# A hybrid encoder layer on one core: later row stores, weight sums behind the block in front, and another price list for the lane planner

## The chip, the core and the metric

The kernel runs on one core of one Trainium2 chip. The engines are TensorE (PE, with its weight loads PEld), VectorE (DVE), ScalarE (ACT), GpSimd (POOL) and SyncE (SP), whose queue issues all the DMAs that are spoken of here. Each engine works off its own queue in the order in which the program wrote it. Times are device microseconds (us) of one execution; the metric is the median of several.

## The reference

One layer of a bidirectional encoder, all in fp32, on two groups of rows: 256 rows of a prompt and 1024 of a sample, together 1280 rows of 2048 features.

```python
def layer(x, mem, ...):
    hn = rms_norm(x, norm_g)
    proj = hn @ w_in                                  # 2048 -> 4896
    xbc, z_ssd, dt_raw, q, k, v, z_att, mq, z_mem = split_cols(proj, IN_SIZES)
    xbc = silu(centred_dwconv(xbc, conv_w, conv_b))
    ...                                               # two SSD scans, forward and backward
    o_ssd = rms_norm(y * silu(z_ssd))
    o_att = window_attention(q, k, v, sink) * silu(z_att)
    mk, mv = split_cols(rms_norm(mem, mem_norm_g) @ w_mem_kv, (512, 512))
    o_mem = (softmax over memory of mq, mk) @ mv * silu(z_mem)
    return x + concat([o_ssd, o_att, o_mem]) @ w_out  # 2048 -> 2048
```

Most of the arithmetic is in the three projections with w_in, w_mem_kv and w_out.

## The kernel before

**Split products.** PE's one-pass type is f32r. Each fp32 operand is split in two such parts: `wsplit` (line 337 of the kernel before) writes the high part `h` with a Copy on ACT and the rest `l` with a subtraction on DVE, and notes both instructions in `marks`. A product is then three matmuls, h·xH, h·xL and l·xH (or l and xL exchanged). In the trace the weights are `wraw` (as loaded), `wh` and `wl`; the rows of x are `ra` and `rb_` (as loaded), `xH` and `xL` (split).

**Stages.** The rows come in two groups of 640. The work goes through PE in this order, with the times of the trace:

1. Two blocks `mk` and `mv` from the memory rows (to about 75 us).
2. The block `q` of group 1 (to 153.5 us). A block takes 16 weight tiles of 128x512, five row tiles each. Beside it run the `p_step`s, which prepare the rows for the next stage: `p_load` (two loads of x), `p_fill` (norm on DVE, split to xH and xL, and two stores `rowH`, `rowL` of each of 16 row tiles to DRAM, from where a later stage reads them back), `p_sums` (four DVE subtractions), `p_split` (tH, tL of these sums).
3. `seven_stage(1)` (to about 423 us): ten units, each eight steps `k`, in which two blocks of weights and rows are multiplied with seven products in place of eight. This needs sums of weights: `weight_sums` loads a tile, makes four POOL operations (`ws`) and queues the result; `block_pair` splits tile and sums (`wh`, `wl` and `sh`, `sl`) and issues the matmuls. The five banks `acc` that the block in front has filled must be evicted (`qs`) before the third and later products can start.
4. Blocks `kv` and `q` of group 0 (to 495 us), then `seven_stage(0)` (to about 741 us).
5. The lanes (760 to about 1460 us): attention, SSD and memory work in small pieces, laid between the matmuls of six further blocks.
6. Blocks of w_out, and the seven-product stage of w_out from 1588 us to the end.

During the seven-product stages one `next(squares)` at four steps of a unit loads a piece of x to `sst` and squares it on ACT for the norm of group 0. Its tile and the first two weight tiles of a pair share a place in memory.

**What sets the order.** The instructions of an engine are put in order by a scheduler from priorities and simulated readiness; `tc.issue_after(ins)` makes what follows stand behind `ins`, but only on the engine of `ins`. So the `marks` bind ACT and DVE and not SP. The loads of the first two weight pairs are issued in `p_step` 23 and 25, ahead of the `issue_after` there. In the lane stage the order on PE is set by a planner, `Clocks`: `cost` gives each instruction a time, `ran` keeps a clock for each engine and the time at which each tile is full, and `ready` lets a lane go on when its inputs are due at most 300 ns (`AHEAD`) after PE's clock:

```python
at = [self.full.get(self.name(x), 0.0) - (0 if n else AHEAD) for x in tiles]
...
return max(at) <= self.now["PE"]
```

Every engine instruction of the kernel's own is recorded under one line of the recording helper, 128 (131 after the change), so groups are told apart by the names of their tiles.

Of the kernel before, what the change touches and what calls it, by code (L numbers as in the profile page):

```python
# [10 lines left out]
F32 = mybir.dt.float32  # L11
# [14 lines left out]
HP = (30, 100, 100)  # L26
# [5 lines left out]
RATES = {'kv': (4, 4), 'mq0': (8, 8), 'z0': (8, 8), 'z1': (8, 8), 'mq1': (8, 8), 'o': (8, 8)}  # L32
DEBT = 6.0
AHEAD, QUEUE = 300.0, 4000.0
NEG = -1e30

UNITS = (0, 4, 1, 5, 2, 6, 7, 3, 8, 9)
# [5 lines left out]
class Clocks:  # L43
# [17 lines left out]
    def cost(self, e, ins, ops, power):  # L61
        n = max([self.size(x) for x in ops] or [1])
        if e == "PE":
            m = self.size(ops[0])
            one_pass = ops[-1].dtype == F32R or ops[1].dtype == F32R
            return m / 2.4 + 14 if one_pass else max(m / 0.6, 213) + 6
        if e == "DVE":
            return 150 + 1.05 * n
        if e == "ACT":
            return (190 + 0.8 * n if n > 16 else 190) + (190 if len(ins.outs) > 1 else 0)  # L70
        if e == "POOL":
            return 60 + 4.2 * n if n > 16 else 250 + 180 * n if power else 300
        return 50

    def ran(self, e, ins, power=False):
        outs, srcs = [[x.bass_ap for x in xs if hasattr(x, "bass_ap")] for xs in (ins.outs, ins.ins)]
        cost = self.cost(e, ins, outs + srcs, power)
        if e != "SP":
            self.now[e] = max(self.now[e], self.now["PE"])
        if not self.lane:  # L80
            self.now[e] += cost
            return
        at = self.now[e] if e != "SP" else self.now["PE"]
        for x in srcs:
            at = max(at, self.full.get(self.name(x), 0.0))
        for x in outs:
            at = max(at, self.free.get(self.name(x), 0.0))
        if e == "SP":
            end = at + 2600 + self.size(outs[0]) * 1.5
        else:  # L90
            end = self.now[e] = at + cost + 20
        for x in srcs:
            k = self.name(x)
            self.free[k] = max(self.free.get(k, 0.0), end)
        for x in outs:
            k = self.name(x)
            if e != "SP":
                self.free[k] = max(self.free.get(k, 0.0), end)
            self.full[k] = end + 90
# [51 lines left out]
def hymba_encoder_kernel(  # L151
# [8 lines left out]
    V, A, G, T, S = [Timed(clk, n, e) for n, e in (("DVE", nc.vector), ("ACT", nc.scalar), ("POOL", nc.gpsimd),  # L160
                                                  ("PE", nc.tensor), ("SP", nc.sync))]
# [69 lines left out]
    row_d = [[dram([P, 640], f"row{n}{k}") for n in "HL"] for k in range(KT)]  # L231
# [28 lines left out]
            lanes[lane].append(((fn.__name__, t), fn(t)))  # L260

    marks = []

    def step(i):
        name, gen = lanes[i][0]
# [45 lines left out]
    cur = {}  # L311
# [31 lines left out]
    def w_laid(src, n):  # L343

        def load(k, raw):
            S.dma_start(raw, src[k])
        return load, n

    def laid_in(name):
# [861 lines left out]
    raw, sums, rows = {}, {}, {}  # L1211
# [46 lines left out]
    for k in range(8):  # L1258
        at = 2 * k - 5 if k < 4 else 4 * k - 13 if k < 7 else 13

        end = 16 if k == 7 else at
# [64 lines left out]
    def block_pair(src, u, rows_of, begin, lead=1):  # L1326

        ps = {p: (acc.tile([P, 512], F32, tag="acc", name="acc") if i < 5 else psum("accm"))[:, :320]
              for i, p in enumerate(seven)}
        parts = {}  # L1330
        for k in range(8):
            weight_sums(src, 8 * u + k + lead)
            with tc.high_priority(offset=HP[2]):
                raw, sums = ahead.pop(0)
                h = [wp.tile([P, 512], F32R, tag="wh", name="wh", bufs=WB),
                     fin.tile([P, 384], F32R, tag="sh", name="sh", bufs=3)]
                l = [wp.tile([P, 512], F32R, tag="wl", name="wl", bufs=WB),
                     fin.tile([P, 384], F32R, tag="sl", name="sl", bufs=3)]
                wsplit(raw, h[0], l[0])
                wsplit(sums, h[1], l[1])  # L1340
            parts[k] = h, l
            if k == 2:
                evac = begin(u)
            if k == 6:
                continue
            ks = (6, 7) if k == 7 else (k,)
            for p, (i, m, c) in seven.items():
                for k_ in ks:
                    h, l = [x[i][:, m * P:(m + 1) * P] for x in parts[k_]]
                    xh, xl = rows_of(k_, p, c)  # L1350
                    T.matmul(ps[p], h, xh, start=(k_ == 0), stop=False)
                    T.matmul(ps[p], h, xl, start=False, stop=False)
                    T.matmul(ps[p], l, xh, start=False, stop=(k_ == 7))
                if k == 7:
                    with tc.high_priority(offset=HP[2]):
                        evac(p, ps[p])
            yield k
# [20 lines left out]
    def p_fill(k, grp):  # L1378

        for i, x in enumerate(raw[k]):  # L1380
            g_ = R_G + k + 8 * i
            V.scalar_tensor_tensor(out=x, in0=x, scalar=vec[:, g_:g_ + 1], in1=rbc, op0=ALU.mult, op1=ALU.mult)
            h, l = new_place(k + 8 * i)
            A.activation(h, x, AF.Copy)
            V.tensor_sub(l, x, h.bitcast(F32))
            if grp == 1:
                for d, y in zip(row_d[k + 8 * i], (h, l)):
                    S.dma_start(d, y.bitcast(F32))

    def p_sums(k):  # L1390
        a, b = [hv(x, 2) for x in raw[k]]
# [19 lines left out]
    def p_step(j, grp):  # L1411
        if j == (3, 9)[grp]:
            need(x_rows, [1 - grp])
        if j in (23, 25):
            weight_sums(w_in_pairs, (j - 23) // 2)
        with ExitStack() as st:
            for ins in marks:
                st.enter_context(tc.issue_after(ins))
            for f, k, *args in sorted(p_plan[grp].get(j, ()),
                                      key=lambda x: ((p_split, p_sums, p_fill, p_load).index(x[0]), x[1])):  # L1420
                f(k, *args)
# [168 lines left out]
    def distances(_):  # L1590
# [7 lines left out]
        V.scalar_tensor_tensor(out=dist, in0=dist, scalar=-1.0, in1=dist, op0=ALU.mult, op1=ALU.min)  # L1598
        G.affine_select(out=dist, in_=dist, compare_op=ALU.is_ge, fill=NEG, base=0,
                        pattern=[[1, 384]], channel_multiplier=-1)  # L1600
# [50 lines left out]
    def one_left():  # L1651
        if left:
            some_left()
# [11 lines left out]
    def seven_stage(grp):  # L1665
        owe = 0.0
        for u, unit in enumerate(units):
            for k in block_pair(w_in_pairs, u, rows_in, ev_seven(*unit, grp), lead=2):
                if k in (0, 2, 4, 5):
                    next(squares, None)  # L1670
                owe = owe + 1.15 if left else 0.0
                while owe >= 1:
                    owe -= 1
                    one_left()
                if u == 0:
                    p_step(32 + k, grp)

    def both(k, j):
        one_left()
# [180 lines left out]
```

## Time and profile before

| what | value |
|---|---|
| median of 3 runs | 1793.35 us (1791.46 to 1794.4) |
| the profiled execution | 1788.47 us |
| its span (first to last instruction) | 1786.8 us |
| PE busy | 1762.2 us, 99% |
| DVE, ACT, POOL busy | 1302.3, 974.9, 668.4 us |
| DMA | 313.23 MB, mean 175 GB/s |

The profile lists an instruction as its start, its length, engine, line, operation, the tile written <- the tiles read, the shape and, in brackets, how long the engine stood idle before it and what ended that. "x2" stands for two of the same in a row. A time in brackets is idle time of that engine alone; for the kernel's time only PE's count directly, with 99% of the span. A stretch of the span is listed with its length, the busy time of the engines, the granted clock of PE (1.00 is full), the mean share of time in which the DMA engines were busy, and GB/s. Because matmuls are pipelined, a matmul's length there is longer than the distance from one to the next.

### The profile page before, as it was taken

The numbers are of one execution on the slowest core, as the hardware profiler recorded it, in microseconds if no ns is written. First come the engines' busy times: TensorE is split into PE (matmuls) and PEld (weight loads), VectorE is DVE, ScalarE is ACT, GpSimd is POOL, SyncE is SP. The second block draws the span as 40 slices with busy tenths as digits, with TensorE's granted clock in tenths as the row PEclk, the third lists the DMA queues.
The fourth block names the chain that finished last, engine by engine and source line by source line (L and its number), as shares of the span: only waits on it lengthen the run. The fifth ranks groups of instructions, "written<-read, shape, count | busy, mean of one in ns | idle before, by whom it ended". The sixth has DMA issues, their size and how long they took to land.

```text
span 1786.8 us, 30971 instructions
## 1 busy us (share of the span) xinstructions
PE 1762.2 (99%) x10306; PEld 1574.1 (88%) x10306; DVE 1302.3 (73%) x2417; ACT 974.9 (55%) x2181; POOL 668.4 (37%) x1092
## 2 busy tenths in 40 slices
PE   9999999999999999999999999999999999999999
PEld 7778999999799999988778877877788888889999
DVE  5585788888958888787788777768776533766665
ACT  6554545554454444346778766657886533433433
POOL 0105788970158889421111001121110100058775
PEclk9999999999999999999999999999999999999999
DMA  8795454455443333366557876666885635644442
GB/s 297 236 309 177 140 140 144 127 146 180 146 148 106 103 118 109 100 200 199 155 162 243 258 248 185 218 199 221 249 254 164 207 115 149 209 136 147 148 142 78
DMA packets 210993, 313.23 MB, mean 175 GB/s; under 512 B 21584, under 2 KB 84368, under 8 KB 210832
## 3 DMA queue, kind: packets, MB, share of 16 engines
q1 hardware_dynamic: 210688, 311.19, 56.1%
q8 instruction: 81, 1.33, 0.3%
q14 instruction: 80, 0.66, 0.1%
q10 hardware_dynamic: 144, 0.06, 0.0%
HBM read 242.42 MB, written 68.75 MB: 174 GB/s over the span
## 4 chain that ended last, share of the span: by engine, by line
PE 81%; issue 6%; DMA 5%; DVE 4%; ACT 2%; POOL 1%; SPq 0%; DVEq 0%; ACTq 0%; POOLq 0%
PE acc L128 58%; PE accm L128 11%; PE py L128 2%; PE psc L128 1%; PE po L128 1%; DVE wl L128 1%; PE pst L128 1%; PE ppt L128 1%; DMA rf<-ac 1%; PE pmo L128 1%; PE pms L128 1%; PE pyf L128 1%; PE pyb L128 1%; DMA wraw<-in_w_in_pairs_dram 1%; DMA rb<-ac 0%
## 5 line engine op out<-in xcount | busy, mean ns | idle before, releaser
L128 PE MATMUL acc<-wh,xH 128*128 128x512 f32 (+1 forms) x1248 | 490.7, 394 | 4.2 <-ACT wh L128 3.7
L128 DVE TENSOR_TENSOR wl<-wraw,wh 128x512 fp32r<-128x512 f32 (+1 forms) x480 | 353.1, 740 | 173.9 <-ACT wh L128 169.8
L128 PE MATMUL acc<-wl,xH 128*128 128x512 f32 (+1 forms) x1248 | 475.1, 381 | 2.8 <-DVE wl L128 2.6
L128 PE MATMUL acc<-wh,xL 128*128 128x512 f32 (+1 forms) x1248 | 472.6, 379 | 0.0
L128 ACT ACTIVATE wh<-wraw 128x512 fp32r<-128x512 f32 (+1 forms) x480 | 291.7, 614 | 200.4 <-PE acc L128 125.7
L128 POOL TENSOR_TENSOR ws<-wraw 128x128 f32<-128x128 f32 x224 | 144.7, 646 | 400.4 <-DMA wraw<-in_w_in_pairs_dram 202.9
L128 PEld LDWEIGHTS acc<-wh,xH 128*128 128x128 f32 x1248 | 234.9, 188 | 51.1 <-issue 7.0
L128 PEld LDWEIGHTS acc<-wl,xH 128*128 128x128 f32 x1248 | 235.2, 188 | 48.7 <-issue 6.5
L128 PEld LDWEIGHTS acc<-wh,xL 128*128 128x128 f32 x1248 | 234.6, 188 | 44.5 <-issue 1.0
L128 ACT ACTIVATE sh<-ws 128x384 fp32r<-128x384 f32 x224 | 116.3, 524 | 275.6 <-POOL ws L128 132.3
L128 DVE TENSOR_TENSOR sl<-ws,sh 128x384 fp32r<-128x384 f32 x224 | 157.1, 704 | 136.8 <-ACT sh L128 134.8
L128 POOL TENSOR_TENSOR ws<-wraw,ws 128x128 f32<-128x128 f32 x224 | 153.4, 685 | 17.3
L128 POOL TENSOR_TENSOR ws<-ws,wraw 128x128 f32<-128x128 f32 x224 | 152.8, 682 | 0.0
L128 POOL TENSOR_TENSOR wraw<-wraw 128x128 f32<-128x128 f32 x224 | 134.9, 602 | 17.3
L128 PE MATMUL acc<-xH,wl 128*128 128x320 f32 x320 | 100.1, 313 | 1.7 <-DVE wl L128 1.4
L128 PE MATMUL acc<-tH,sh 128*128 128x320 f32 x320 | 99.1, 310 | 1.9 <-ACT qs L128 1.9
L128 PE MATMUL acc<-tH,sl 128*128 128x320 f32 x320 | 99.2, 310 | 0.0
L128 PE MATMUL acc<-xL,wh 128*128 128x320 f32 x320 | 98.9, 309 | 0.0
L128 PE MATMUL accm<-tH,wl 128*128 128x320 f32 x320 | 98.8, 309 | 0.0
L128 PE MATMUL acc<-xH,wh 128*128 128x320 f32 x320 | 98.7, 309 | 0.0
L128 PE MATMUL accm<-tL,wh 128*128 128x320 f32 x320 | 98.7, 308 | 0.0
L128 PE MATMUL accm<-tH,wh 128*128 128x320 f32 x320 | 98.7, 308 | 0.0
(458 smaller groups left out, 3833.0 us busy)
## 6 DMA issues: line engine op xcount, KB each, us to landing
wraw<-in_w_in_pairs_dram SPq DMA_DIRECT2D x160, 256.0 KB, 2.7
wraw<-in_w_in_laid_dram SPq DMA_DIRECT2D x128, 256.0 KB, 3.6
wraw<-in_w_out_laid_dram SPq DMA_DIRECT2D x64, 256.0 KB, 3.0
wraw<-in_w_out_pairs_dram SPq DMA_DIRECT2D x64, 256.0 KB, 2.9
rf<-ac SPq DMA_DIRECT2D x40, 256.0 KB, 3.8
rb<-ac SPq DMA_DIRECT2D x40, 256.0 KB, 4.1
wraw<-in_w_mem_laid_dram SPq DMA_DIRECT2D x32, 256.0 KB, 4.4
ra<-in_x_turned_dram SPq DMA_DIRECT2D x16, 320.0 KB, 3.2
```

Source lines behind the costliest of these rows:

```text
L128: r = f(*a, **kw)
```

## The change

1. **Prices of the planner.** A vector operation of n columns costs 67 + 1.04 n ns in place of 150 + 1.05 n; a scalar one 50 (from PSUM) or 92 (from SBUF) + 0.835 n, in place of 190 + 0.8 n, and 92 for each further operand or accumulated output. The engine's clock goes on by that cost, and the result is there 90 (DVE) or 110 ns (ACT) later. Matmuls of more than one pass cost in proportion to their partitions.
2. **First weight sums.** `p_step` 23 and 25 issue the loads and sums of the first two weight pairs behind the `marks` and behind the last load of a laid weight block (`raws`, on SP).
3. **First splits of a seven-product stage.** In its unit 0, for k < 3, the splits are issued behind the marks of the block in front.
4. **Row stores.** `p_fill` issues none; `keep_rows` issues them one by one in units 2 to 9 of `seven_stage(1)`, behind `marks`.
5. **Squares.** At unit 0 and k = 0 and 2, no `next(squares)`.

```diff
+LATE = {"ACT": 110.0, "DVE": 90.0}
...
         if e == "PE":
...
-            return m / 2.4 + 14 if one_pass else max(m / 0.6, 213) + 6
+            return m / 2.4 + 14 if one_pass else max(m / 0.6, 213) * list(ops[0].ap)[0][1] / 128 + 6
         if e == "DVE":
-            return 150 + 1.05 * n
+            return 67 + 1.04 * n
         if e == "ACT":
-            return (190 + 0.8 * n if n > 16 else 190) + (190 if len(ins.outs) > 1 else 0)
+            aps = sum(hasattr(x, "bass_ap") for x in ins.ins)
+            return (50 if ops[-aps].space == "PSUM" else 92) + 0.835 * n + 92 * (aps - 1) + (92 if len(ins.outs) > 1 else 0)
...
-            end = self.now[e] = at + cost + 20
+            self.now[e] = at + cost
+            end = at + cost + LATE.get(e, 20)
...
     marks = []
+    raws = [None]
...
         def load(k, raw):
-            S.dma_start(raw, src[k])
+            raws[0] = S.dma_start(raw, src[k]).ins
...
+        front = tuple(marks) if u == 0 else ()
         for k in range(8):
             weight_sums(src, 8 * u + k + lead)
-            with tc.high_priority(offset=HP[2]):
+            with ExitStack() as st:
+                st.enter_context(tc.high_priority(offset=HP[2]))
+                for ins in front if k < 3 else ():
+                    st.enter_context(tc.issue_after(ins))
                 raw, sums = ahead.pop(0)
...
             V.tensor_sub(l, x, h.bitcast(F32))
-            if grp == 1:
-                for d, y in zip(row_d[k + 8 * i], (h, l)):
-                    S.dma_start(d, y.bitcast(F32))
...
-        if j in (23, 25):
-            weight_sums(w_in_pairs, (j - 23) // 2)
         with ExitStack() as st:
             for ins in marks:
                 st.enter_context(tc.issue_after(ins))
+            if j in (23, 25):
+                st.enter_context(tc.issue_after(raws[0]))
+                weight_sums(w_in_pairs, (j - 23) // 2)
...
-                if k in (0, 2, 4, 5):
+                if k in (0, 2, 4, 5) and (u or k > 2):
                     next(squares, None)
+                if grp == 1 and 2 <= u < 10 and k in (0, 2, 4, 7):
+                    keep_rows(4 * (u - 2) + (0, 2, 4, 7).index(k))
...
+    def keep_rows(i):
+
+        with ExitStack() as st:
+            for ins in marks:
+                st.enter_context(tc.issue_after(ins))
+            k, n = divmod(i, 2)
+            S.dma_start(row_d[k][n], cur["HL"[n], k].bitcast(F32))
```

What this does to the written order is seen at three places.

SP at the end of the q block of group 1, before and then after. `rowH_`, `rowL_` are the row stores, `wraw<-in_w_in_laid_dram` loads of the q block's weights, `wraw<-in_w_in_pairs_dram` loads for the seven-product stage, `sst` the first piece for the squares:

```order
L128 DMA rowH_224<-xH_1466 128x640
L128 DMA rowL_225<-xL_1467 128x640
L128 DMA rb__1473<-in_x_turned_dram 128x640
L128 DMA rowH_210<-xH_1519 128x640
L128 DMA rowL_211<-xL_1520 128x640
L128 DMA wraw<-in_w_in_laid_dram 128x512 x2
L128 DMA rowH_226<-xH_1526 128x640
L128 DMA rowL_227<-xL_1527 128x640
L128 DMA wraw<-in_w_in_pairs_dram 128x512 x4
L128 DMA sst<-in_x_sample_dram 128x512
L128 DMA q_143<-qs 128x512
```

The same place on SP after the change (the store `rowL_227`, a fourth pair load and `sst` follow):

```order
L131 DMA rowH_210<-xH_1491 128x640
L131 DMA rowL_211<-xL_1492 128x640
L131 DMA wraw<-in_w_in_pairs_dram 128x512
L131 DMA rowH_220<-xH_1268 128x640
L131 DMA rowL_221<-xL_1269 128x640
L131 DMA rowH_222<-xH_1335 128x640
L131 DMA wraw<-in_w_in_pairs_dram 128x512
L131 DMA rowL_223<-xL_1336 128x640
L131 DMA rowH_224<-xH_1440 128x640
L131 DMA wraw<-in_w_in_pairs_dram 128x512
L131 DMA rowL_225<-xL_1441 128x640
L131 DMA rowH_226<-xH_1496 128x640
```

All 32 row stores still stand ahead of the stage; the four pair loads, which stood behind them all, now stand among them.

ACT at the join between that q block and `seven_stage(1)`, before and then after. `wh` are weight splits, `sh` splits of weight sums, `qs` the evictions of the q block, `sst,xs` a Square:

```order
L128 ACTIVATE wh<-wraw 128x512
L128 ACTIVATE xH_1526<-rb__1473 128x640
L128 ACTIVATE wh<-wraw 128x512 x2
L128 ACTIVATE sh<-ws 128x384
L128 ACTIVATE tH<-ra 128x640
L128 ACTIVATE tH<-rb__1400 128x640
L128 ACTIVATE wh<-wraw_1388 128x512
L128 ACTIVATE qs<-acc 128x512 x2
L128 ACTIVATE sst,xs_1754<-sst 128x512
L128 ACTIVATE qs<-acc 128x512 x2
L128 ACTIVATE wh<-wraw_1451 128x512
L128 ACTIVATE wh<-wraw 128x512
```

The same join on ACT after the change:

```order
L131 ACTIVATE wh<-wraw 128x512 x4
L131 ACTIVATE sh<-ws 128x384 x3
L131 ACTIVATE wh<-wraw_1364 128x512
L131 ACTIVATE tH<-ra 128x640
L131 ACTIVATE qs<-acc 128x512
L131 ACTIVATE tH<-rb__1376 128x640
L131 ACTIVATE qs<-acc 128x512
L131 ACTIVATE sst,xs_1846<-sst 128x512
L131 ACTIVATE qs<-acc 128x512 x2
L131 ACTIVATE wh<-wraw_1427 128x512
L131 ACTIVATE wh<-wraw 128x512
L131 ACTIVATE qs<-acc 128x512
```

The splits `wh` of the q block now stand together ahead of all three `sh`; the Square stands between the second and the third eviction in both.

ACT at the join between the q block of group 0 and `seven_stage(0)`, with the same names, before and then after:

```order
L128 ACTIVATE wh<-wraw 128x512
L128 ACTIVATE sh<-ws 128x384
L128 ACTIVATE tH<-ra 128x640
L128 ACTIVATE xH_5816<-rb__5765 128x640
L128 ACTIVATE wh<-wraw 128x512
L128 ACTIVATE tH<-rb__5692 128x640
L128 ACTIVATE wh<-wraw 128x512
L128 ACTIVATE wh<-wraw_5674 128x512
L128 ACTIVATE qs<-acc 128x512 x2
L128 ACTIVATE sst,xs_4856<-sst 128x512
L128 ACTIVATE qs<-acc 128x512 x2
```

The second join on ACT after the change:

```order
L131 ACTIVATE wh<-wraw 128x512
L131 ACTIVATE xH_5811<-rb__5760 128x640
L131 ACTIVATE wh<-wraw 128x512 x2
L131 ACTIVATE sh<-ws 128x384 x3
L131 ACTIVATE wh<-wraw_5669 128x512
L131 ACTIVATE tH<-ra 128x640
L131 ACTIVATE qs<-acc 128x512
L131 ACTIVATE tH<-rb__5687 128x640
L131 ACTIVATE qs<-acc 128x512
L131 ACTIVATE sst,xs_6117<-sst 128x512
L131 ACTIVATE qs<-acc 128x512 x2
```

The two last `wh` of the q block, which stood behind `sh` and two `tH`, now stand ahead of them.

## The prediction

> **What bounds the kernel now.** I read the head of the page first, then the waits of PE, then the clock by stretch, and only then single instructions. TensorE (PE) is busy nearly all the time:
>
> ```profile
> span 1786.8 us, 30971 instructions
> PE 1762.2 (99%) x10306; PEld 1574.1 (88%) x10306; DVE 1302.3 (73%) x2417; ACT 974.9 (55%) x2181; POOL 668.4 (37%) x1092
> ```
>
> So there are 1786.8 − 1762.2 = 24.6 us of PE idle time, and no edit here removes a matmul. What can be won is a part of that idle time, and time that PE spends at a lower clock. The waits of PE over the whole span, largest first (total, times, longest), say where it idles, and the stretches below them (length, then busy time of PE, PEld, DVE, ACT, POOL, then granted clock, DMA share, GB/s) say where the clock fell:
>
> ```profile
> PE acc L128 <- DVE wl L128: 4.0, 6, 1.4
> PE acc L128 <- ACT wh L128: 3.7, 3, 1.6
> PE acc L128 <- ACT qs L128: 1.9, 1, 1.9
> PE ppt L128 <- DVE nm L128: 1.4, 1, 1.4
> ...
> 110.00:115.00 5.00, 3.53 (x16) 2.60 (x15) 2.61 (x4) 1.37 (x2) 0.00 (x0) 1.00 0.99 333
> 155.00:160.00 5.00, 3.47 (x12) 3.07 (x13) 1.30 (x2) 4.04 (x10) 0.02 (x1) 0.66 0.68 234
> 490.00:495.00 5.00, 4.30 (x11) 3.21 (x12) 1.91 (x3) 1.18 (x3) 3.55 (x7) 0.66 0.52 149
> 760.00:1590.00 830.00, 820.38 (x4385) 672.85 (x4384) 591.56 (x1290) 525.21 (x1344) 94.26 (x174) 1.00 0.64 199
> ```
>
> The reader is to see two things. The three largest waits are for the weight split (wh, wl) and for one eviction (qs). And in two stretches, which are the joins between a q block and the seven-product stage behind it, the clock is 0.66: (1 − 0.66) × 5 = 1.7 us is lost at each on top of the wait. The long lane stage idles 830 − 820.38 = 9.6 us, in a dozen small waits.
>
> [...]
>
> **Part A: the mk block (53 us).** PE waits twice there, because ACT stands at the sum split sh, which waits for POOL's weight sums of the first pair, and the block's own wh stands behind it:
>
> ```profile
> 52.00 0.53 ACT L128 ACTIVATE sh<-ws 128x384 fp32r<-128x384 f32 x1 [2.94 <-POOL ws L128]
> ...
> 53.09 0.50 PE L128 MATMUL acc<-wh,xH 128*128 128x512 f32 x1 [0.65 <-ACT wh L128]
> 54.28 0.50 PE L128 MATMUL acc<-wl,xH 128*128 128x512 f32 x1 [0.69 <-DVE wl L128]
> ```
>
> In the new order of ACT no sh stands in this block. The wh goes 2.94 us earlier at least in part; the gain is 0.65 + 0.69 = 1.34, with bounds 0 (another wait just behind) and 1.34. The two loads and eight POOL operations go to the q block instead. POOL has the room (gap of 73.66 us in the row under part C).
>
> **Part B: the q block (112 us).**
>
> ```profile
> 106.11 0.32 SPq L128 DMA_DIRECT2D rowL<-xL  x1
> 106.96 0.96 SPq L128 DMA_DIRECT2D wraw<-in_w_in_laid_dram  x1
> 111.71 0.63 ACT L128 ACTIVATE wh<-wraw 128x512 fp32r<-128x512 f32 x1 [3.19 <-DMA wraw<-in_w_in_laid_dram]
> 112.40 1.19 PE L128 MATMUL acc<-wh,xH 128*128 128x512 f32 x4 [1.47 <-ACT wh L128]
> ...
> rowL<-xL SPq DMA_DIRECT2D x16, 320.0 KB, 3.7
> ```
>
> The weight load is issued only after the row stores ahead of it on SP, which themselves wait for their splits, and it lands 4.75 us after issue, on a DMA that is 99% busy. In the new order this load stands ahead of those stores: −1.47. Against it: the 32 stores don't go to the seven-product stage. On SP they all still stand ahead of the first sst load and the q stores, and behind the last load of x there are now 14 of them where there were 4. Ten stores of 320 KB at 333 GB/s (row above) are 9.6 us of DMA time that comes later, in a stretch that has some 0.19 × 25 = 4.8 us free:
>
> ```profile
> 125.00:150.00 25.00, 25.00 (x112) 20.71 (x111) 17.79 (x31) 10.43 (x17) 4.07 (x8) 1.00 0.81 272
> ```
>
> The excess of about 5 us reaches the join unless the stores, which nobody waits for, give way to the loads. Bounds of B: −1.47 to +1.4 (a second wait like this one). I take −1.47, because most stores stand behind the loads that matter. The Squares that are dropped at the first unit go later into the seven-product stage, on an ACT that is busy 55% of the span (head of the page): 0, and without that cover 0.63 each (row at 155.15 below).
>
> **Part C: the first join (154 us).**
>
> ```profile
> 145.61 0.46 POOL L128 TENSOR_TENSOR ws<-wraw 128x128 f32<-128x128 f32 x1 [73.66 <-DMA wraw<-in_w_in_pairs_dram]
> 147.61 0.53 ACT L128 ACTIVATE sh<-ws 128x384 fp32r<-128x384 f32 x1 [3.41 <-POOL ws L128]
> 149.30 0.62 ACT L128 ACTIVATE wh<-wraw 128x512 fp32r<-128x512 f32 x1
> 155.15 0.63 ACT L128 ACTIVATE sst<-sst 128x512 f32<-128x512 f32 x1 [4.26 <-DMA sst<-in_x_sample_dram]
> 155.77 1.07 ACT L128 ACTIVATE qs<-acc 128x512 f32<-128x512 f32 x2
> 150.88 0.94 DVE L128 TENSOR_TENSOR wl<-wraw,wh 128x512 fp32r<-128x512 f32 x1
> 137.67 0.32 SPq L128 DMA_DIRECT2D rowL<-xL  x1
> 141.41 3.87 SPq L128 DMA_DIRECT2D wraw<-in_w_in_pairs_dram  x4
> 151.90 0.33 SPq L128 DMA_DIRECT2D sst<-in_x_sample_dram  x1
> 153.29 0.39 PE L128 MATMUL acc<-wh,xL 128*128 128x512 f32 x1
> 154.25 0.31 PE L128 MATMUL acc<-xH,wl 128*128 128x320 f32 x1
> 156.40 0.55 PE L128 MATMUL acc<-tH,sh 128*128 128x320 f32 x1 [1.85 <-ACT qs L128]
> ```
>
> Read backwards: PE waits for the third eviction (qs at 155.77); that stands behind a Square, which waits for its tile sst; the load of sst goes out at 151.90, when wl (150.88 + 0.94 = 151.82) has freed the buffer that both share; and wl waits for wh at 149.30, which stands behind sh and its POOL sums. The Square still stands between the second and third eviction afterwards. But the pair load that feeds the late sums is now issued among the stores instead of behind them all, so I put it at 138 instead of 141.41 (between the store at 137.67, behind which it now stands, and no change). Sums and sh come some 3.4 us earlier; wh is then held only by PE's release of a wh buffer (about 146.7: the 30 matmuls of the last two weights, 0.23 us apart by the rows at 487, before the block's end at 153.5), wl ends near 148.5, the load of sst goes out near 148.6 and, by the 3.25 us that it took (155.15 − 151.90), lands near 151.9. Square and the third eviction end near 153.1, ahead of PE's need at 154.4. Gain: 1.85 of idle time and 1.7 of clock, 3.55 in all. Bounds 0 and 3.55.
>
> **Part D: the second join (490 us).**
>
> ```profile
> 483.76 0.53 ACT L128 ACTIVATE sh<-ws 128x384 fp32r<-128x384 f32 x1 [3.28 <-POOL ws L128]
> 488.59 0.74 ACT L128 ACTIVATE tH<-rb__5692 128x640 fp32r<-128x640 f32 x1 [2.52 <-DVE rb__5692 L128]
> 489.23 1.14 ACT L128 ACTIVATE wh<-wraw 128x512 fp32r<-128x512 f32 x2
> 487.67 0.39 PE L128 MATMUL acc<-wl,xH 128*128 128x512 f32 x1
> 487.90 0.39 PE L128 MATMUL acc<-wh,xL 128*128 128x512 f32 x1
> 489.90 0.50 PE L128 MATMUL acc<-wh,xH 128*128 128x512 f32 x1 [1.62 <-ACT wh L128]
> 491.11 0.79 PE L128 MATMUL acc<-wl,xH 128*128 128x512 f32 x1 [0.70 <-DVE wl L128]
> ```
>
> The last weights of the q block (wh at 489.23) stand behind sh, two xH/tH splits and a wait for DVE. In the new ACT order the last two wh of the block stand ahead of the three sh and of the last two tH. That removes 1.62 + 0.70, and the clock's 1.7: 4.02. What is late next is sh and the tH splits, whose first reader on PE stands behind the 30 matmuls of the last two weights, 30 × 0.23 = 6.9 us; without that cover the 2.52 of the row at 488.59 would come back. Bounds 0 and 4.02. At the third join (the first w_out pair) the order of ACT does not change: 0.
>
> **Part E: the lanes.** The new estimate prices a 512-column vector operation at 67 + 1.04 × 512 = 599 ns of engine time and 689 until its result; the old one at 688 and 708. Rows of the lane stage (count, busy, mean ns):
>
> ```profile
> L128 DVE TENSOR_TENSOR state<-state,cd_all 128x512 f32<-128x512 f32 x24 | 16.4, 682 | 0.0
> L128 ACT ACTIVATE zs<-acc 128x512 f32<-128x512 f32 x20 | 11.8, 592 | 3.7 <-PE acc L128 3.7
> ```
>
> For an eviction of 512 columns it gives 50 + 427 + 110 = 587. So the new results' times fit the rows (682 and 592) within about 1%, and the lane matmuls move forward: 50 to 70 block matmuls by the order of PE, at 0.23 us each 11 to 16 us. Both queues have room (591.56 and 525.21 busy of 830). PE does the same matmuls and can only win or lose idle time: half of the 9.6 us gone is −5, doubled is about +9. I take 0, as an estimate that fits leaves the same margin of 300 ns that the planner had.
>
> **Sum.** 1.34 + 1.47 + 3.55 + 4.02 + 0 = 10.4. The profiled execution took 1788.47 (span 1786.8 and 1.67 around it), so 1778.1 for its like. The median of the runs, 1793.35, lies 4.9 above it: 1783.0.
>
> **The rivals.**
> - *The lanes wait more* (the other side). PE takes its matmuls in order, so each one placed before its input is ready stops all. For: the list of waits there consists of lane inputs (nm above, 1.4). Against: the fit of the prices. It decides when the lane idle time grows by over 10.4 + 3.6 = 14 us; at about 1 us each that is 14 new waits. It would give some 1797. Chance 0.08.
> - *The first join is not cured*: the Square stands where it stood and its load now follows a crowd of stores. For: the excess of 5 us; if sst lands 2 us later than I put it, the third eviction is late again. 1783 + 3.55 = 1786.5. Chance 0.17.
> - *The stores stay in the q block and crowd it*: part B gives nothing and one more wait of 1.4 comes: 1783 + 2.9 = 1785.9. For: the order of SP, and a DMA share of 0.99. Chance 0.13.
> - *The clock does not come back*: the half clock at the joins hangs on something else than these gaps (a gap of 1.47 at 112 us left it at 1.00): 1783 + 3.4 = 1786.4. Chance 0.03.
>
> [...]
> - *The lanes wait less*: 1778. Chance 0.1.
>
> **How the numbers follow.** The forecast has 0.49. Range: from 1776.5, a little under the lanes' gain, to 1790.5, where the second and third rivals come together with a loss of a few us in the lanes; only the first rival lies wholly outside. A difference of 0.2% (3.6 us) is what can be told: under 1789.8 is faster, above 1796.9 slower. All cases but the first rival end under 1789.8 taken alone (0.92); the spread of the median (1791.46 to 1794.4 now) and rivals that come together move 0.12 of it to no change, and the first rival gives 0.07 slower: 0.80, 0.13, 0.07.
>
> **What would show it.** A: no sh and no PE wait near 53 us. B: the wait at 112 us gone, and no other above 1 us up to 150. C: a clock of 1.00 around 155 us, with sst landed before 153. D: the same around 490. E: idle time of 7 to 12 us in the lane stage. The forecast is wrong if the clock is still 0.66 at a join, if the q block shows a new wait for a weight load, or if the lane idle time passes 15 us.

## The result, and the profile after

The change makes the kernel slower: 1801.06 us (1800.0 to 1804.0) against 1793.57 before, a ratio of 1.0047 with a 95% interval of 1.0034 to 1.0061. I had forecast 1783.0 and faster. The head of the page of the kernel after, and PE's longest waits over its span:

```profile
span 1801.4 us, 30978 instructions
PE 1766.0 (98%) x10306; PEld 1576.4 (88%) x10306; DVE 1311.5 (73%) x2417; ACT 972.1 (54%) x2181; POOL 683.7 (38%) x1092
```

```profile
PE pxs L131 <- DMA xc<-xbc_d: 4.7, 2, 3.7
PE po L131 <- ACT pT L131: 3.1, 2, 2.3
PE acc L131 <- ACT qs L131: 2.7, 3, 1.3
PE psc L131 <- ACT pT L131: 2.6, 2, 1.4
PE pacs L131 <- DVE dtw L131: 2.4, 1, 2.4
PE acc L131 <- DVE yt L131: 2.3, 2, 1.3
PE psc L131 <- DVE moT L131: 2.2, 1, 2.2
...
PE acc L131 <- ACT wh L131: 0.3, 1, 0.3
```

The weight splits, which led the list before (wl 4.0, wh 3.7), are gone from its head. The inputs of lane matmuls have taken their place. The two profiled executions side by side, each stage from its first block matmul on PE to that of the next stage (us):

| stage | before | after | difference |
|---|---|---|---|
| mk, mv and q blocks | 148.1 | 144.2 | −3.9 |
| first seven-product stage | 252.3 | 247.8 | −4.5 |
| kv and q blocks | 92.9 | 87.2 | −5.7 |
| second seven-product stage | 246.3 | 249.3 | +3.0 |
| lanes and w_out blocks | 838.9 | 865.0 | +26.0 |
| third seven-product stage | 198.8 | 198.6 | −0.2 |

Up to the start of the lanes the change wins 11.2 us (745.0 to 733.8); my sum said 10.4. This holds beyond the one profile: in the seventeen with edits 2 to 5 that are shown below the lanes begin between 732.8 and 736.9 us, in the two without them at 745.0 and 746.7. All of the gain, and more, is lost again in the lane stage. Stretches of the kernel after, with the columns of the prediction's fence:

```profile
49.00:54.00 5.00, 5.00 (x24) 4.14 (x23) 1.37 (x2) 1.48 (x3) 0.00 (x0) 1.00 0.80 247
112.00:117.00 5.00, 5.00 (x24) 4.14 (x23) 5.00 (x9) 3.50 (x6) 2.72 (x2) 1.00 0.96 316
152.00:157.00 5.00, 4.98 (x34) 4.98 (x35) 3.29 (x7) 2.91 (x7) 1.24 (x3) 1.00 0.53 194
485.00:490.00 5.00, 2.87 (x18) 2.30 (x17) 1.29 (x2) 3.74 (x8) 1.54 (x4) 1.00 0.55 210
733.80:1598.80 865.00, 839.49 (x4471) 688.82 (x4470) 595.44 (x1300) 526.42 (x1351) 95.03 (x170) 0.99 0.62 191
```

At 53 and 112 us PE is full, and at 152 us it is full again behind a last wait of 0.60; the clock is 1.00 in all three. At the second join (485 us) the clock is 1.00 as well, but PE is idle for 2.1 us of the five. In the lane stage PE is idle 865.0 − 839.49 = 25.5 us, where the same stage before had 838.9 − 830.5 = 8.4. The rest of the 26.0 is clock: in the lanes of this trace the clock is 0.50 from 807.14, 967.57 and 1203.09 us for 3.41 us each and from 1022.18 for 6.83, together 17.1 us at half clock, which cost 8.5 us, and in the kernel before it is 0.50 nowhere in this stage. The lane stage of the kernel before:

```profile
745.00:1583.90 838.90, 830.52 (x4470) 683.57 (x4469) 594.80 (x1299) 527.92 (x1351) 91.71 (x170) 1.00 0.64 197
```

Three of the 21 waits of this stage, followed back. First the matmul on PE, then the queue of the engine that it waits for:

```profile
967.31 1.75 PE L131 MATMUL po<-pT,v_all 128*64 128x256 f32 x6 [2.32 <-ACT pT L131]
...
964.05 1.28 ACT L131 ACTIVATE rf<-rf,wj_all 128x128 f32<-128x128 f32 x4 [1.85 <-DMA rf<-ac]
966.48 0.40 ACT L131 ACTIVATE rf<-rf,wj_all 128x128 f32<-128x128 f32 x1 [1.15 <-DMA rf<-ac]
966.79 0.85 ACT L131 ACTIVATE pT<-ppt 128x384 f32<-128x384 f32 x2
...
1202.85 0.51 PE L131 MATMUL psc<-kT,qT 128*128 128x384 f32 x1 [2.19 <-DVE moT L131]
...
1201.77 0.69 DVE L131 TENSOR_TENSOR q<-q,qr 128x512 f32<-128x512 f32 x1 [2.33 <-POOL qr L131]
1202.38 0.75 DVE L131 TENSOR_TENSOR moT<-pmo,zm 128x256 f32<-128x256 f32 x2
...
1016.10 0.58 SPq L131 DMA_DIRECT2D xc<-xbc_d  x1
1023.39 0.72 PE L131 MATMUL pxs<-identr,xc 128*128 128x128 f32 x4 [3.70 <-DMA xc<-xbc_d]
```

In the first, pT is ready to be evicted, but on ACT it stands behind an operation on `rf` whose load has not landed: the two loads of `rf` that ACT waits for took 4.0 and 4.6 us from issue to landing. In the second, moT stands on DVE behind an operation that waits for POOL. In the third, a load itself is late: issued at 1016.10, it landed 7.2 us later. None of them is a vector or scalar operation that took longer than its price. The three make 8.2 of the 25.5 us; the other waits were not followed back.

### The profile page after: what moved, and what is told of

Read it like the earlier page. It is cut to its first block, busy times and chain, and to the rows that moved or that the text cites. A ratio compares the mean times of both kernels' runs of the same rounds, so it can differ in the third digit from the quotient of the medians.

```text
span 1801.4 us, 30978 instructions
## 1 busy us (share of the span) xinstructions
PE 1766.0 (98%) x10306; PEld 1576.4 (88%) x10306; DVE 1311.5 (73%) x2417; ACT 972.1 (54%) x2181; POOL 683.7 (38%) x1092
## 4 chain that ended last, share of the span: by engine, by line
PE 82%; DVE 7%; DMA 6%; ACT 2%; issue 2%; POOL 1%; SPq 0%; DVEq 0%; ACTq 0%
PE acc L131 60%; PE accm L131 11%; PE py L131 2%; DVE wl L131 1%; DMA rf<-ac 1%; PE psc L131 1%; PE po L131 1%; PE pst L131 1%; PE pms L131 1%; PE pmo L131 1%; PE ppt L131 1%; DMA xc<-xbc_d 1%; PE pyb L131 1%; DMA rb<-ac 1%; DVE rb L131 1%
## 5 line engine op out<-in xcount | busy, mean ns | idle before, releaser
L131 POOL TENSOR_TENSOR ws<-wraw 128x128 f32<-128x128 f32 x224 | 152.6, 681 | 394.9 <-ACT rH L131 168.2
L131 POOL TENSOR_TENSOR es<-sinkb,nm 128x2 f32<-128x2 f32 x40 | 13.3, 333 | 226.5 <-DVE nm L131 197.1
```

The source lines that it names most:

```text
L131: r = f(*a, **kw)
```

## The experiments

All kernels compute the whole layer. The lane stage is given as length and PE's idle time in it, both from the profile; the position of the lane matmuls is their mean shift on PE against the kernel before, counted in block matmuls (minus is earlier), from the written order. A stage length is that of one profile, and half clock in it makes it longer (some 3.4 us in e8, none in e1, by mean clocks of 0.998 and 1.000 over the span). The kernel before, run beside each set, had medians of 1791.8 to 1793.7, so the ratio compares better than the time.

| kernel | shift | lane stage, idle (us) | time (us) | ratio, 95% interval |
|---|---|---|---|---|
| before | 0 | 838.9, 8.4 | 1793.4 | |
| after | −56 | 865.0, 25.5 | 1801.1 | 1.0034 to 1.0061 |
| e1 old prices | 0 | 840.3, 9.9 | 1779.4 | 0.9905 to 0.9943 |
| e2 prices only | −56 | 858.9, 23.2 | 1813.0 | 1.0092 to 1.0142 |
| e3 vector price old | +36 | 848.7, 16.1 | 1791.5 | 0.9976 to 1.0006 |
| e4 new, AHEAD −300 | −6 | 842.2, 11.5 | 1780.4 | 0.9913 to 0.9958 |
| e5 PE price new | +25 | 854.7, 18.0 | 1793.0 | 0.9989 to 1.0013 |
| e6 vector price new | −84 | 853.4, 16.7 | 1795.8 | 1.0001 to 1.0030 |
| e7 scalar price new | −2 | 853.3, 18.4 | 1791.2 | 0.9975 to 1.0003 |
| e8 old, no Square at joins | 0 | 842.0, 8.8 | 1777.1 | 0.9889 to 0.9942 |
| e9 old, AHEAD 350 | −4 | 845.7, 13.3 | 1784.0 | 0.9920 to 0.9950 |
| e10 old, AHEAD −300 | +58 | 848.1, 15.2 | 1787.8 | 0.9955 to 0.9990 |
| e11 new, AHEAD −400 | +28 | 860.4, 22.0 | 1798.7 | 1.0014 to 1.0050 |
| e12 scalar new, AHEAD −300 | +52 | 838.8, 7.6 | 1780.2 | 0.9901 to 0.9942 |
| e13 new, slow loads | +34 | 853.7, 17.6 | 1789.8 | 0.9974 to 1.0000 |
| e14 scalar new, slow loads | +72 | 843.4, 12.2 | 1781.3 | 0.9916 to 0.9953 |
| e15 PE new, slow loads | +89 | 841.4, 9.8 | 1781.1 | 0.9917 to 0.9953 |
| e16 vector new, slow loads | −30 | 851.3, 17.0 | 1789.1 | 0.9964 to 0.9993 |
| e17 e8, stores as before | 0 | 840.5, 10.2 | 1785.0 | 0.9950 to 0.9977 |
| e18 e8, stores truly later | 0 | 839.4, 9.2 | 1777.4 | 0.9897 to 0.9934 |

**Which half of the change costs: e1 and e2.** e1 is the change with the old prices:

```diff
-            return m / 2.4 + 14 if one_pass else max(m / 0.6, 213) * list(ops[0].ap)[0][1] / 128 + 6
+            return m / 2.4 + 14 if one_pass else max(m / 0.6, 213) + 6
-            return 67 + 1.04 * n
+            return 150 + 1.05 * n
... (the scalar price likewise)
-            self.now[e] = at + cost
-            end = at + cost + LATE.get(e, 20)
+            end = self.now[e] = at + cost + 20
```

> The change with the planner's old prices: edits 2 to 5 alone; the lane matmuls stand where they stood before. Theory (the lane loss comes from the prices alone, which put the lane matmuls on average 56 block matmuls earlier on PE): the joins and the q block keep the 11.2 us that the two profiles show up to the start of the lanes, the lane stage goes back from 865 to about 839 us, so some 11 us under the kernel before, about 1782. Rival (the lane stage pays for edits 2 to 5, because it starts earlier against its loads or with other row stores): the lane stage stays well above 845 us and the time at about 1800.

e2 makes the opposite edit: the same lines, the other way round, in the kernel before.

> The kernel before with the new prices alone. Theory: the lane stage loses all of its 26 us (17 of idle time and some 8.5 of half clock), nothing is won ahead of it: about 1793.5 + 26 = 1819. Rival: the prices alone cost under 8 us, about 1794 to 1801.

The lane stages of e1 and of e2:

```profile
734.60:1574.90 840.30, 830.45 (x4471) 684.09 (x4470) 595.50 (x1300) 526.39 (x1351) 91.81 (x170) 1.00 0.64 197
```

```profile
746.70:1605.60 858.90, 835.67 (x4470) 685.38 (x4469) 594.50 (x1300) 526.13 (x1350) 94.72 (x170) 1.00 0.62 193
```

With the old prices the stage is back at 840.3 us and the kernel at 1779.4, 14 us under the one before. The prices alone cost 20.0 us there and 19.6 in time (I expected 26). So the prices are the loss, and edits 2 to 5 the gain: 19.6 − 14.0 = 5.6 us, where the whole change costs 7.5.

**Which price: e3, e5, e6, e7.** Each has edits 2 to 5. e3 is the change with `return 150 + 1.05 * n` for DVE and its result 20 ns later, as before; the other three are e1 with one price of the change:

```diff
e5 -            return m / 2.4 + 14 if one_pass else max(m / 0.6, 213) + 6
e5 +            return m / 2.4 + 14 if one_pass else max(m / 0.6, 213) * list(ops[0].ap)[0][1] / 128 + 6
e6 -            return 150 + 1.05 * n
e6 +            return 67 + 1.04 * n      (result 90 later)
e7 -            return (190 + 0.8 * n if n > 16 else 190) + (190 if len(ins.outs) > 1 else 0)
e7 +            the change's scalar price  (result 110 later)
```

> The change with the old price and the old result time for vector operations alone (150 + 1.05 n, plus 20); the other new prices stay. On PE the lane matmuls then stand 36 block matmuls later than in the kernel before. Theory (the surplus in the old vector price was the margin of the lanes): lane idle time at or under that of before (8.4 us), no half clock, time 1778 to 1784. Rival (the loss hangs on the scalar price or on that of the matmuls of several passes): the lane stage stays above 855 us, the time near 1800.

> Edits 2 to 5 with the old prices, except that matmuls of several passes are priced by their partitions. Lane matmuls stand 25 block matmuls later on PE than before the change. Theory A (how far forward the lane matmuls stand decides): lane stage 836 to 841 us, time 1776 to 1780. Theory B (the old prices of PE and of the vector engine were both too high and stood against each other; any one of them put right alone makes the order worse, as the old vector price did in the kernel that kept the other new prices): lane stage 846 to 852 us, time 1786 to 1791.

> Edits 2 to 5 with the old prices, except that vector operations have the new price and result time. Lane matmuls stand 84 block matmuls earlier than before the change, farther than with all the new prices (56). Theory A: the lanes lose more than the 26 us of the full change: lane stage 870 to 885 us, time 1810 to 1825. Theory B: also worse than the old prices, by some 26 to 40 us. Against both: a lane stage of 840 to 850 us would say that the vector price is not what costs.

> Edits 2 to 5 with the old prices, except that scalar operations have the new price and result time. Lane matmuls stand where they stood (1.5 block matmuls earlier on average). Theory A: no loss, lane stage 838 to 843 us, time 1778 to 1782. Theory B (a margin in the scalar price guarded the matmuls that wait for the scalar engine, such as psc and po behind pT): lane stage 845 to 852 us, time 1785 to 1791.

Each single price makes the lane stage 13 to 14 us longer than the old prices do, whether the lane matmuls stand 25 later, 84 earlier or, with the scalar price, where they were on average. e3, with the old vector price and matmuls 36 later, still waits 16.1 us. My theory, that the loss grows with how much earlier the matmuls stand, falls. The lane stage of e6, the farthest move:

```profile
735.10:1588.50 853.40, 836.67 (x4470) 685.95 (x4469) 592.48 (x1300) 527.20 (x1350) 99.43 (x170) 0.99 0.63 194
```

**More margin: e4, e9 to e12.** The edit in each is one number:

```diff
-AHEAD, QUEUE = 300.0, 4000.0
+AHEAD, QUEUE = -300.0, 4000.0   (e4 in the change, e10 in e1, e12 in e7; e9: 350 in e1; e11: -400 in the change)
```

> The change with all its prices, but a lane goes on only when its inputs were due 300 ns ago, in place of up to 300 ns ahead (AHEAD -300 for 300). On PE the lane matmuls stand 6 block matmuls earlier than before the change on average, in place of 56. Theory (placement decides, by whatever means): most of the lane loss goes, lane idle time 8 to 14 us, time 1782 to 1790. Rival (an order of work made by the new prices that is bad in itself, or loads that come late, not the distance from an input to its matmul): still above 1796.

> Edits 2 to 5 with the old prices and a margin that is a little smaller: inputs may be due 350 ns ahead instead of 300. Lane matmuls stand 4 block matmuls earlier on PE on average, so every distance is nearly as it was, but the order is another one. Theory C (the order under the old prices was the one of many that happens to wait little, and any other costs some 13 us, as the three single prices did: 853 to 855 us of lane stage): 848 to 858 us, time 1788 to 1795. Theory D (the distance from an input to its matmul decides, and the single prices took some of it for their own engine's inputs): 839 to 845 us, time 1778 to 1784.

> Edits 2 to 5 with the old prices and 600 ns more margin: a lane goes on only when its inputs were due 300 ns ago. Lane matmuls stand 58 block matmuls later on average. Theory C: another order, so 848 to 858 us of lane stage, time 1788 to 1795. Theory D: more margin everywhere, 835 to 842 us, time 1774 to 1781.

> The whole change with its new prices and AHEAD at -400, 100 ns more margin than the kernel with -300 that came to a lane stage of 842 us. Theory C (842 was a chance find): 850 to 865 us, time 1788 to 1803. Theory D (with the true prices it is the margin that counts): 836 to 843 us, time 1775 to 1782.

> Edits 2 to 5, old prices except the new one for scalar operations, and AHEAD at -300. With 300 this kernel had a lane stage of 853 us, idle 18.4 us. Theory C: no different, 848 to 858 us, time 1786 to 1793. Theory D: the 600 ns take away most of the extra waits, 838 to 845 us, time 1777 to 1784.

e4 seemed to settle it: 600 ns more margin gave 842.2 us. But 100 ns more than that (e11) gave 860.4, and the same 600 ns under the old prices made the stage 7.8 us longer (e10 against e1), under the new scalar price 14.5 us shorter (e12 against e7). Neither margin nor position predicts the sign. A small change of margin (e9) costs 5.4 us, between what theories C and D said, and no more than two profiles of one order can differ (6.1, next). The same order repeats better than orders agree: before, e1, e8, e17 and e18 share one and lie at 838.9 to 842.0 us, the change and e2 share another at 865.0 and 858.9, and the thirteen further orders lie at 838.8 to 860.4.

**The price of loads: e13 to e16.** The loads that lanes wait for, in the kernel after between 760 and 1400 us (count, KB, median us from issue to landing):

```profile
rf<-ac SPq DMA_DIRECT2D x40, 256.0 KB, 4.1
rb<-ac SPq DMA_DIRECT2D x40, 256.0 KB, 4.3
...
xc<-xbc_d SPq DMA_DIRECT2D x18, 256.0 KB, 5.0
```

The planner gives each of them 2600 + 1.5 × 512 = 3368 ns, before and after the change. The edit, in the change (e13), e7 (e14), e5 (e15) and e6 (e16):

```diff
-            end = at + 2600 + self.size(outs[0]) * 1.5
+            end = at + 4600 + self.size(outs[0]) * 1.5
```

> The whole change with its new prices, and the planner's price of a DMA raised by 2.0 us (4600 + 1.5 n ns in place of 2600 + 1.5 n; for 512 columns 5.4 us in place of 3.4, where the loads xc, rb and rf took 5.0, 4.3 and 4.1 in the median). Theory E (the lanes wait because loads land later than the planner allows, and engines that stand in order behind such a load hold up others): lane stage 838 to 847 us in place of 865, time 1776 to 1786. Theory C (any new order gives a draw from the same 839 to 865 us, mean 851): around 851 us, time around 1790, and the four kernels of this set together as wide apart as the ten before.

> Edits 2 to 5, old prices except the new one for scalar operations, and DMAs priced 2.0 us higher. Without the latter the lane stage was 853 us. Theory E: 836 to 845 us, time 1775 to 1784. Theory C: a draw around 851 us, time around 1790.

> Edits 2 to 5, old prices except the new one for matmuls of several passes, and DMAs priced 2.0 us higher. Without the latter the lane stage was 855 us. Theory E: 836 to 845 us, time 1775 to 1784. Theory C: a draw around 851 us, time around 1790.

> Edits 2 to 5, old prices except the new one for vector operations, and DMAs priced 2.0 us higher. Without the latter the lane stage was 853 us. Theory E: 838 to 847 us, time 1776 to 1786. Theory C: a draw around 851 us, time around 1790.

All four stages got shorter: by 11.3, 9.9, 13.3 and 2.1 us, and in the ratios all four kernels are faster than without the edit, with intervals that don't touch. Two fall into theory E's range (843.4, 841.4), and these are the two with the old vector price. The two with the new one stay at 853.7 and 851.3. But the four don't decide between E and C. They began from orders that were worse than most, so that a mere new draw would help too: the eleven orders with the old price of loads have a mean of 850 us, these four one of 847, and by an estimate from those eleven, draws among the other ten would all four come out shorter about one time in three. That loads land later than they are priced is seen directly in two of the waits above (4.0, 4.6 and 7.2 us, against 3.4); that a right price makes a good order is not shown, nor that the vector price's surplus covers something else, which two kernels against two suggest. Against a simple sum stands that the old prices, with the low price of loads, wait as little as the best of these.

**The row stores and the Square: e8, e17, e18.** e8 is e1 without Squares in the first unit; e17 is e8 with the stores issued in `p_fill` again, as before the change; e18 is e8 with the stores bound on SP behind the latest pair load, so that they really go out in units 2 to 9:

```diff
e8  -                if k in (0, 2, 4, 5) and (u or k > 2):
e8  +                if u and k in (0, 2, 4, 5):
e17 +            if grp == 1:
e17 +                for d, y in zip(row_d[k + 8 * i], (h, l)):
e17 +                    S.dma_start(d, y.bitcast(F32))
e17 -                    keep_rows(4 * (u - 2) + (0, 2, 4, 7).index(k))
e18 +        pairs[0] = S.dma_start(raw, src[i // 8, i % 8]).ins
e18 +            st.enter_context(tc.issue_after(pairs[0]))
```

> Edits 2 to 5 with the old prices, and no Square is issued in the whole first unit of a seven-product stage, so none stands between the second and the third eviction at a join. What this tells: whether the two new waits for the evictions at the second join (1.31 and 0.82 us, a loss of 2.4 us) and the one of 0.60 at the first come from the Square, whose piece lands late. If so, both joins run through: 3.0 us less than the same kernel with the Square there (1779.4), about 1776.5. Rival (the evictions are late because the splits tH wait for the sums on DVE): the same waits stay, about 1779.

> The kernel without Squares at the joins and with the old prices (e8, 1777.1 us), with edit 4 undone: p_fill issues the row stores again. The lane matmuls stand where they stand there. If the gain of 1.47 us at 112 us comes from edit 4: that wait comes back, and the q block is 1.5 us longer, about 1778.6. If it comes from the edits 2 and 3 alone: 1777 and no wait above 1 us in the q block. My prediction's part B says the first.

> The same kernel (e8) with the row stores bound behind the pair loads on SP, so that they really go out in units 2 to 9 of the first seven-product stage, where the change in words wants them. If stores among the loads cost something in the q block or at the join: up to 1 us less than e8 ahead of that stage. If they are hidden anyway: the same, 1776 to 1778. Rival on the other side: in the seven-product stage they hold up pair loads and its length grows beyond 249.5 us.

In e8 the waits for evictions at the joins fall to one of 0.3 us in all, from 0.60 at the first and 1.31 + 0.82 at the second in the kernel after (2.8 in all in e1). So the Square made them. The time is 2.3 us under e1 where I said 3.0, but the intervals overlap, and in the two profiles the lanes begin only 1.0 us earlier: what this is worth is not shown. The two long waits of PE ahead of the lanes in e17:

```profile
111.41 1.21 PE L129 MATMUL acc<-wh,xH 128*128 128x512 f32 x4 [2.02 <-ACT wh L129]
146.54 1.63 PE L129 MATMUL acc<-wh,xH 128*128 128x512 f32 x4 [2.56 <-ACT wh L129]
```

```profile
111.00:116.00 5.00, 4.59 (x14) 3.67 (x15) 4.60 (x6) 2.76 (x5) 1.00 (x2) 0.70 0.86 298
146.00:151.00 5.00, 4.46 (x13) 3.51 (x14) 3.71 (x5) 3.01 (x6) 3.05 (x5) 0.66 0.50 154
```

Without edit 4 the kernel is 7.9 us slower than e8 (1785.0 to 1777.1): the wait at 111 us is there again, a second one of 2.56 comes at the end of the block, and each costs a stretch at half clock. I had said 1.5 us. So the edit carries more than half of what e8 gains over the kernel before (0.0049 of 0.0085 in the ratios). How far back the stores then go counts for nothing more. The stretch from 125 to 150 us in e8, and then in e18:

```profile
125.00:150.00 25.00, 25.00 (x114) 20.84 (x113) 16.66 (x24) 12.39 (x22) 10.33 (x16) 1.00 0.85 311
```

```profile
125.00:150.00 25.00, 25.00 (x112) 20.70 (x111) 17.62 (x25) 11.59 (x20) 8.96 (x14) 1.00 0.39 119
```

With the true move the DMA share there is 0.39 instead of 0.85 in e8, and the times are the same (1777.4 and 1777.1): the stores that stayed were hidden.

## Why the prediction was wrong

**Part A, right.** No sh and no wait stand at 53 us. A and B together were to bring 2.8 us up to the first join; they brought 3.9. Most of the further 1.1 lies in how a wait is listed: a matmul of 512 columns is listed 0.39 us long, but its neighbours start 0.23 apart, so PE loses more than the listed idle time. Counted from start to start, the three waits of the kernel before cost 3.6 us instead of 2.8. The last 0.3 is not traced.

**Part B, right in its sign and its edit, too small in what the edit is worth.** The wait at 112 us is gone, on a DMA that is still 96% busy. e17 shows that without edit 4 the other edits would not have kept that gain and would have met a second wait, which I had not priced. Its rival, stores that crowd the block, did not come.

**Part C, right in its sequence, with some luck in the number.** I put the load of sst at 148.6 us and the third eviction ahead of PE's need; the times are earlier by the 3 to 4 us of A and B, and the sequence is the one that I worked out. PE runs through the third product at full clock, and a wait of 0.60 is left behind it. The first seven-product stage is 4.5 us shorter where I said 3.55, but some 1.6 of that is not the join: the kernel before waits 1.37 us for a wl at 276.7 us, in the middle of the stage, and this profile of the change doesn't. Five others with the same edits (e6, e7, e12, e15, e16) wait 1.2 to 1.3 us at about 270. So the join itself gave about 2.9:

```profile
145.47 0.33 SPq L131 DMA_DIRECT2D sst<-in_x_sample_dram  x1
...
148.75 0.63 ACT L131 ACTIVATE sst<-sst 128x512 f32<-128x512 f32 x1 [1.41 <-DMA sst<-in_x_sample_dram]
149.38 1.07 ACT L131 ACTIVATE qs<-acc 128x512 f32<-128x512 f32 x2
...
150.38 0.31 PE L131 MATMUL acc<-tH,sh 128*128 128x320 f32 x1
152.02 0.41 PE L131 MATMUL acc<-xH,sh 128*128 128x320 f32 x1 [0.60 <-ACT qs L131]
```

**Part D, half right.** Both waits and the half clock are gone, but I named the wrong thing as late next. I wrote of sh and tH; it was the Square, as at the first join, whose load waits for the buffer that wl frees (wl ends at 482.22 us, the load goes out at 482.29):

```profile
482.29 0.33 SPq L131 DMA_DIRECT2D sst<-in_mem_prompt_dram  x1
...
485.55 0.63 ACT L131 ACTIVATE sst<-sst 128x512 f32<-128x512 f32 x1 [1.40 <-DMA sst<-in_mem_prompt_dram]
...
486.81 0.41 PE L131 MATMUL acc<-tH,sh 128*128 128x320 f32 x1 [1.31 <-ACT qs L131]
488.82 0.42 PE L131 MATMUL acc<-xH,sh 128*128 128x320 f32 x1 [0.82 <-ACT qs L131]
```

The kv and q blocks gave 5.7 us and the next stage took 3.0 back: 2.7 net where I said 4.0. I had read this chain at the first join and not asked whether the second has the same. The full clock there isn't owed to shorter gaps alone. In e13 the same two waits (1.23 and 0.82) are followed by half clock, in the kernel after (1.31 and 0.82) they are not; and e1, e3, e4, e12, e14 and e15, which have this join too, show a mean clock of 1.000 over their whole span. The stretch in the kernel after, and then in e13:

```profile
488.00:493.00 5.00, 4.18 (x28) 4.18 (x29) 3.98 (x8) 2.37 (x6) 0.91 (x2) 1.00 0.51 181
```

```profile
488.00:493.00 5.00, 4.32 (x19) 4.33 (x20) 3.74 (x7) 1.78 (x4) 0.89 (x2) 0.66 0.54 169
```

That parts A to D together came so near (11.2 for 10.4) is in part luck: A, B and C brought more than I said, D less.

**Part E, the step that failed.** I took 0 "as an estimate that fits leaves the same margin of 300 ns". It cost 26 us, beyond the +9 of my bound. Three things were wrong in it. I tested the prices on the durations of single operations, where they do fit, and took that for a test of the order that the planner makes of them. (They fit as engine time too: vector operations of 512 columns that stand back to back in the lane stage follow each other at a median of 602 ns, priced 599.) What moved the matmuls should be this engine time and hardly the result time that I compared (argued from the prices; no run parts the two): by the line `end = self.now[e] = at + cost + 20` the old price held the engine for 708 ns, not the 688 that I wrote, so by the new price each such operation frees its engine 109 ns sooner, but gives its result only 19 ns sooner. The three waits above come from queues behind late loads and behind a POOL result (its three operations took 2.2 us, which the planner prices at 2.3, so this one was not late by its price), and I had not looked at the price of a load (3.37 us, against 4.1 to 5.0 in the median). I also took the idle time before (8.4 us in this stage) as what any order of this planner has. It is not: of the fifteen kernels with another order, one had less. The old order was one of the best of those tried, and every edit of the estimate made another one. And for the lanes I priced only idle time: a third of the loss (8.5 of 26.0 us) is half clock, at the four waits of 2.19 to 3.70 us.

The first rival had the mechanism, and its point of decision was right: the lane idle time grew by 17 us, over the 14 that I had named, and the kernel became slower. It said some 1797, and 1801.1 came. Its chance of 0.08 was far too low, and the range left it out. What remains open is why one order waits 8 us and another 25. Position and margin don't say it, and the price of loads may say a part of it.

The clock at the first join came back from 0.66 to 1.00 when the gap of 1.85 us went, as I had reckoned from the row.

## What to carry to other kernels

Where an estimate only sets an order, a better estimate isn't yet a better order: price what the order does (who stands behind whom, and which load is under it), make a few orders of about the same quality to learn their spread, and treat the present one as chosen from them. Split a change that has a local half and a global half before judging it; here the local half alone is 0.8% faster. When a wait is removed at a join, follow the whole chain at every place of the same shape.

## What the hardware showed

Some waits of PE were followed by half clock and others were not. In the lanes of the kernel after, the waits of 2.44 us ahead of 806.82, of 2.32 ahead of 967.31 and of 2.19 ahead of 1202.85 were, with half clock from 807.14, 967.57 and 1203.09; in the one of 3.70 that ends at 1023.39 half clock began at 1022.18, with the wait still on. The next longest there, of 1.55 ahead of 899.70 and of 1.38 ahead of 1278.93, left the clock at 1.00. But in e2 a wait of 2.66 us, longer than three of the four that were followed by half clock, left it at 1.00 as well, and at the second join two waits of nearly the same lengths ended both ways (part D). So in these traces the length of a wait alone doesn't say whether half clock follows; what does is not shown. The stretch of the kernel after, then the gap and the stretch of e2:

```profile
1202.00:1207.00 5.00, 4.15 (x10) 2.81 (x11) 3.86 (x10) 0.72 (x2) 0.19 (x1) 0.66 0.38 106
```

```profile
1034.36 0.51 PE L131 MATMUL pxs<-identr,xc 128*128 128x128 f32 x4 [2.66 <-DMA xc<-xbc_d]
1030.00:1041.00 11.00, 8.29 (x45) 6.49 (x44) 6.37 (x14) 3.58 (x9) 0.00 (x0) 1.00 0.97 337
```
